# Tying a depthwise convolution's taps to fixed places in VectorE's queue

## The chip, the cores and the metric

The kernel runs on one core of one Trainium2 chip. A core has five engines that work side by side, each with its own queue that it works off in order: TensorE (matrix products; PE in the profile, PEld for its weight loads), VectorE (DVE), ScalarE (ACT), GpSimd (POOL) and SyncE (SP, which issues the DMAs here). The metric is the device time of one execution in microseconds.

## What is computed

Two layers of a block with three branches that share one input projection: sparse attention with 8 heads in 2 groups, retention with 4 heads, and a convolution. A gated sum of the three, an output projection and a feed-forward part follow. The sequence has 512 positions, the width is 1024, everything is float32. The part that the change touches is the convolution branch: 512 channels, 31 taps, causal, one weight per channel and tap.

```python
def _conv_module(a, b, dw_w, dw_b, ln_g, ln_b):
    u = a * jax.nn.sigmoid(b)
    kern = dw_w[:, None, :].astype(u.dtype)
    y = lax.conv_general_dilated(u, kern, window_strides=(1,), padding=[(CONV_WIDTH - 1, 0)],
                                 dimension_numbers=('NWC', 'WIO', 'NWC'), feature_group_count=CONV_CH)
    y = y + dw_b
    y = _layernorm(y, ln_g, ln_b)
    return jax.nn.silu(y).astype(a.dtype)
```

Between the branches stand

```python
    o_nsa = _nsa(q_n, kc, vc, ks, vs, kw, vw, g_n, ...)
    o_ret = _retention(q_r, k_r, v_r, g_r, ret_gn[l])
    o_conv = _conv_module(c_a, c_b, conv_w[l], conv_b[l], conv_ln_g[l], conv_ln_b[l])
    proj = jnp.einsum('bsnc,ncd->bsnd', br, w_branch[l])
    merged = jnp.sum(gate * proj, axis=2).astype(x.dtype)
```

## The kernel before, in words

Activations are held with features on the 128 partitions and the 512 positions along the free axis. Every product is done in a split form: a float32 operand is cut into a high part (rounded by ScalarE) and a low part (the rest, by VectorE or GpSimd), and three products replace one. `wblock` (L152) loads a weight block by DMA, ScalarE makes the high part `wh` (L144), and GpSimd the low part `wl` (L147), or VectorE in the feed-forward part (L149). All matrix products have line L108.

A layer goes through these stages:

- **Retention** (L336 to L435, "ret" pool). Queries and keys are projected (tiles `mm` and `sc`), rotated block by block on VectorE (L356 to L360, tile `rr`), transposed on TensorE and split (tile `qk`). For each of 4 heads follow: values centred on VectorE (L393 to L395, for the heads 0 and 2), scores on TensorE (tile `sc`), decay (L416, tile `rt`), the split (L111 and L112, tile `pr`), the product with the values (tile `av`), a normalisation (L428, L429) and a split (tile `bo`). After each of the first three heads `conv_input` (L303) projects the input `u` of the next of 4 convolution channel blocks; the first block is projected ahead of retention.
- **Keys** (L474 to L572). Compressed keys and values (`compress`, L482; L496 writes `XP`), the two sets of keys (L551 to L558, tile `kv`) and values (L567) of the attention.
- **Attention** (L644 to L747): 4 head pairs j, each with 2 groups g and 2 branches br, thus 16 units of 4 blocks i, 64 blocks in all. In a unit TensorE makes the scores, VectorE adds the bias and takes the minimum (L705), ScalarE the exponential (L707), VectorE scales the block by the gate over the denominator (L712, tile `s`), TensorE transposes it (L715, tile `tp`), ScalarE and VectorE split the transposed block (L720, L721, tile `pt`), and TensorE multiplies with the values (tile `av`). `more` (L736) adds independent projections between the units (`fill`: gates L444, mixes L460), queued on TensorE behind the first score product of the unit.
- **Post and feed-forward**: mixes of the three branches, output projection, then two large products.

The convolution's output is `yc`, 4 tiles of 128 channels by 512 positions. A **tap** is one VectorE instruction over 128x512 values, `yc = u shifted * weight + yc` (L333; the first tap of a channel block adds the bias, L331). There are 4 x 31 = 124 taps a layer, in a chain for each block. `conv_taps(n)` (L324) issues the next n taps whose input exists: 2 behind each of the 8 rotated blocks, 1 behind each of the 16 score splits, and 2 behind each attention block until none is left. `conv_norm` (L578) normalises the result in four pieces; `more` issues a piece a unit once no tap is left. `mix(2, OC, m)` (L767) uses it after the attention.

What sets the order: the program is built by a list scheduler that keeps, for each engine, a heap of ready instructions with the program's order as priority, and simulates a timeline. An instruction that is ready while nothing of higher priority is goes out early. So the place of `conv_taps(n)` in the program is a priority, and no place in VectorE's queue. `tc.issue_after(ins)` puts the instructions inside it behind `ins` on the queue of the engine that both use, with no wait.

Of the kernel before, what the change touches and what calls it, by code (L numbers as in the profile page):

```python
# [17 lines left out]
P = 128  # L18
# [48 lines left out]
def block_kernel(ctx: ExitStack, tc: tile.TileContext, a, out):  # L67
# [8 lines left out]

    T_ROT, T_SCORE, T_QUERY = 2, 1, 2

# [31 lines left out]
    def split(hi, lo, src, eng=None):  # L110
        nc.scalar.activation(hi, src, AF.Copy)  # L111
        (eng or nc.vector).tensor_sub(lo, src, f(hi))  # L112

# [155 lines left out]
    for l in range(DEPTH):  # L269
# [33 lines left out]
        def conv_input(c):  # L303
# [13 lines left out]
            us.append(u)  # L317

        conv_input(0)
        yc = [tl(cp, "yc", 4) for _ in range(4)]  # L320
# [25 lines left out]
        for which, c0 in (("q", 0), ("k", 2)):  # L346
# [3 lines left out]
            for i in range(NB):  # L350
                z = pz[i].rearrange("p (h s d) -> p h s d", s=2, d=32)
                cosb = cs[:, i, None, None, 0:32].to_broadcast([P, 4, 2, 32])
                sinb = cs[:, i, None, 32:64].to_broadcast([P, 4, 32])
                A = tl(rp, "rr", 8, (P, 4, 2, 32))
                B = tmp((P, 4, 2, 32))
                nc.vector.tensor_mul(A, z, cosb)  # L356
                nc.vector.tensor_mul(B[:, :, 0, :], z[:, :, 1, :], sinb)
                nc.vector.tensor_mul(B[:, :, 1, :], z[:, :, 0, :], sinb)
                nc.vector.tensor_sub(A[:, :, 0, :], A[:, :, 0, :], B[:, :, 0, :])  # L359
                nc.vector.tensor_add(A[:, :, 1, :], A[:, :, 1, :], B[:, :, 1, :])  # L360
                rr.append(A)
                conv_taps(T_ROT)
            for c in range(2):
# [19 lines left out]
        for h in range(4):  # L383
# [26 lines left out]
            for j in range(NB):  # L410
# [5 lines left out]
                nc.vector.tensor_mul(t[:, :n], s[:, :n], dec[:, :n])  # L416
                split(ph[:, at[j]], pl[:, at[j]], t[:, :n])
                conv_taps(T_SCORE)
            o = ps("av")
# [61 lines left out]
        def compress(fb, w1, w2, pe_at, is_k):  # L481
# [12 lines left out]
            for g in range(2):  # L494
                blocks = bass.AP(tensor=E.tensor, offset=E.offset + g * T, ap=[list(E.ap[0]), [2, 16], [16, NCMP]])
                nc.vector.tensor_add(XP[:, :, g, :], blocks, pe[:, :, None].to_broadcast([P, 16, NCMP]))  # L496
            w1t = []
# [49 lines left out]
        for br, fb in ((0, FB_KS), (1, FB_KW)):  # L547
# [4 lines left out]
            for g in range(2):  # L552
                nat, oth = halves(g)
                KHH[br, g], KLL[br, g] = kv(), kv()
                nc.scalar.activation(KHH[br, g][nat], t[nat], AF.Copy)
                nc.scalar.activation(KHH[br, g][oth], t[nat], AF.Copy)
                for half in (nat, oth):
                    nc.vector.tensor_sub(KLL[br, g][half], t[nat], f(KHH[br, g][nat]))  # L558
        G = tl(mix_pool, "G", 1, (P, NB, 24))
# [3 lines left out]
        for i in range(NB):  # L563
            v = kv((P, 4, P))
            zv = pz[i][:, :256].rearrange("p (c d) -> p c d", d=DH)
            nc.scalar.activation(v[:, :, 0:64], zv, AF.Copy, scale=rs4[:, i:i + 1])
            nc.vector.scalar_tensor_tensor(v[:, :, 64:128], zv, rs4[:, i:i + 1], f(v[:, :, 0:64]), op0=OP.mult,  # L567
                                           op1=OP.subtract)
            nc.scalar.activation(G[:, i, :], pz[i][:, 256:280], AF.Tanh, scale=rs4h[:, i:i + 1])
            V.append(v)  # L570
        phase.close()

# [71 lines left out]
        def attention_pair(j, tq, more):  # L644
# [43 lines left out]
            for g in range(2):  # L688
# [4 lines left out]
                for br in range(2):  # L693
# [17 lines left out]
                    for i in range(NB):  # L711
                        nc.vector.tensor_scalar(cols[i], cols[i], c[:, i:i + 1], None, op0=OP.mult)  # L712
                        pt = ps("tp")
                        for k in range(i + 1):
                            nc.tensor.transpose(pt[:, k * P:(k + 1) * P], cols[i][:, k * P:(k + 1) * P], ident)  # L715
                        for (vh, ks), (vl, _) in zip(pt_views(ph, i), pt_views(pl, i)):
# [4 lines left out]
                            nc.vector.tensor_sub(vl, src, f(vh))  # L721
                        conv_taps(T_QUERY)
                    for k, c0 in enumerate((0, 512, 896, 1152)):
# [9 lines left out]

        ON, marks, tqs = [], [], [query(0)]

        def more(j, k):  # L736
# [142 lines left out]
```

## Time and profile before

| | us |
|---|---|
| time, median of 3 runs | 1838.71 (1836.65 to 1839.05) |
| profiled execution | 1835.35 |
| its span, first to last instruction | 1833.6 |
| PE busy in the span | 1759.7 |
| DVE busy | 1162.1 |
| ACT busy | 721.4 |
| POOL busy | 512.0 |

The profiled execution lies 3.4 us below the median, and its span 1.75 us below its own time. The page lists for each engine the time in which it ran anything; a slice table cuts the span in 40 stretches of 45.8 us. A layer takes about 905 us, and its retention, keys and attention lie from 30 to 460 us in the first layer and from 930 to 1365 us in the second. "PEclk" is the share of TensorE's full clock (2.4 GHz) that was granted; 0.5 is the lower level (1.2 GHz).

### The profile page before, as it was taken

The page shows a single profiled execution, that of the slowest core. Times are in us where ns is not written, and L with a number is a line of the kernel's source. Part 1 is how long each engine was busy: PE and PEld are TensorE (multiplying, and loading weights), DVE is VectorE, ACT ScalarE, POOL GpSimd, SP SyncE. Part 2 cuts the span into 40 slices and gives each one's busy share as a digit, 9 for nine tenths or more (in the row PEclk, how much of TensorE's full clock was granted, in tenths as well). Part 3 has the DMA queues.
Part 4 walks back from the last instruction along what each step waited for, and adds up shares of the span by engine and source line. Part 5 has one row for each costly group of instructions (what it writes and reads, how often), then busy time and mean ns, then how long its engine had stood idle before and what let it go on. Part 6 is the DMA issues. An engine that isn't in the chain of part 4 may idle for free.

```text
span 1833.6 us, 23278 instructions
## 1 busy us (share of the span) xinstructions
PE 1759.7 (96%) x8592; PEld 1474.4 (80%) x8592; DVE 1162.1 (63%) x2107; ACT 721.4 (39%) x1293; POOL 512.0 (28%) x420
## 2 busy tenths in 40 slices
PE   8899899999999999999999878999999999999997
PEld 7777788888888888888897767888888888888886
DVE  7999977777554343434479998767766443434344
ACT  4423445566343232323433324555653432313231
POOL 4444433423471000000344544343235700000000
PEclk9999999999999999999999989999999999999998
DMA  4221442322653223233422113233128432232221
GB/s 165 83 74 59 130 150 94 113 87 81 229 167 104 92 92 103 92 94 102 144 81 75 65 58 129 98 110 109 69 81 268 141 97 92 93 103 92 94 91 69
DMA packets 70801, 195.82 MB, mean 107 GB/s; under 512 B 8944, under 2 KB 9328, under 8 KB 70688
## 3 DMA queue, kind: packets, MB, share of 16 engines
q1 hardware_dynamic: 70688, 194.34, 32.2%
q8 instruction: 68, 1.11, 0.2%
q14 instruction: 45, 0.37, 0.1%
HBM read 177.51 MB, written 19.42 MB: 107 GB/s over the span
## 4 chain that ended last, share of the span: by engine, by line
PE 58%; issue 21%; DVE 20%; DMA 1%; ACT 0%; SPq 0%; POOLq 0%; POOL 0%; DVEq 0%; ACTq 0%
PE mm L108 50%; DVE yc L333 9%; PE sc L108 3%; PE av L108 2%; PE tp L715 2%; DVE pr L112 1%; PE tp L108 1%; DVE rt L416 1%; DVE kv L558 1%; DVE qk L381 1%; DVE rr L359 0%; DVE t L395 0%; DVE XP L496 0%; DMA m<-in_cmp_w_k_dram 0%; DVE rr L360 0%
## 5 line engine op out<-in xcount | busy, mean ns | idle before, releaser
L108 PE MATMUL mm<-X,wh 128*128 128x512 f32 x2432 | 772.8, 396 | 17.4 <-ACT X L213 6.2
L147 POOL TENSOR_TENSOR wl<-wr,wh 128x512 fp32r<-128x512 f32 (+2 forms) x344 | 442.2, 1308 | 530.4 <-ACT wh L144 478.9
L144 ACT ACTIVATE wh<-wr 128x1024 fp32r<-128x1024 f32 (+2 forms) x301 | 296.4, 986 | 658.7 <-PE mm L108 554.1
L108 PEld LDWEIGHTS mm<-X,wh 128*128 128x128 f32 x2432 | 455.1, 190 | 108.3 <-ACT X L213 6.2
L108 PE MATMUL mm<-X,wl 128*128 128x512 f32 x1216 | 480.7, 395 | 0.2 <-DVE wl L149 0.2
L108 PEld LDWEIGHTS mm<-X,wl 128*128 128x128 f32 x1216 | 230.6, 190 | 46.8 <-DVE wl L149 0.6
L333 DVE SCALAR_TENSOR_TENSOR yc<-u,ccol,yc 128x512 f32<-128x512 f32 x240 | 227.5, 960 | 1.9
L149 DVE TENSOR_TENSOR wl<-wr,wh 128x1024 fp32r<-128x1024 f32 x129 | 158.1, 1225 | 38.6 <-ACT wh L144 38.6
L108 PE MATMUL mm<-bo,wh 128*128 128x512 f32 x512 | 163.5, 397 | 6.3 <-DVE g L444 5.8
L108 PE MATMUL mm<-fa,wh 128*128 128x512 f32 x512 | 160.2, 395 | 0.0
L796 DVE SCALAR_TENSOR_TENSOR t<-mm,rs 128x512 f32<-128x512 f32 x64 | 43.9, 691 | 161.3 <-PE mm L108 156.0
L205 POOL TENSOR_TENSOR n<-n,mhalf 128x4 f32<-128x4 f32 x15 | 18.1, 1208 | 403.8 <-DVE n L203 403.8
L226 POOL TENSOR_TENSOR t<-t,t 128x512 f32<-128x512 f32 x18 | 27.4, 1524 | 333.6 <-DVE wl L149 314.4
L108 PE MATMUL mm<-kv,wh 128*128 128x512 f32 x384 | 119.5, 389 | 0.0
L108 PEld LDWEIGHTS mm<-bo,wh 128*128 128x128 f32 x512 | 97.5, 191 | 26.8 <-DVE g L444 6.2
L108 PEld LDWEIGHTS mm<-fa,wh 128*128 128x128 f32 x512 | 96.1, 188 | 23.2
L721 DVE TENSOR_TENSOR pt<-tp,pt 128x256 fp32r<-128x256 f32 (+1 forms) x192 | 70.3, 373 | 55.2 <-ACT pt L720 54.7
L108 PE MATMUL mm<-bo,wl 128*128 128x512 f32 x256 | 101.2, 395 | 0.0
L108 PE MATMUL mm<-fa,wl 128*128 128x512 f32 x256 | 100.6, 395 | 0.0
L108 PE MATMUL mm<-wh,X 128*128 128x256 f32 (+1 forms) x480 | 94.5, 295 | 4.2 <-DVE t L307 4.2
L720 ACT ACTIVATE pt<-tp 128x256 fp32r<-128x256 f32 (+1 forms) x192 | 63.9, 343 | 86.0 <-PE tp L715 53.3
L807 DVE TENSOR_TENSOR yc<-yc,mm 128x512 f32<-128x512 f32 x32 | 22.0, 688 | 105.6 <-PE mm L108 105.6
(219 smaller groups left out, 2449.2 us busy)
## 6 DMA issues: line engine op xcount, KB each, us to landing
wr<-in_w_dram SPq DMA_DIRECT2D x128, 512.0 KB, 3.5
wr<-in_w_f_dram SPq DMA_DIRECT2D x87, 512.0 KB, 3.2
wr<-in_w_b_dram SPq DMA_DIRECT2D x48, 256.0 KB, 2.7
wr<-in_w_t_dram SPq DMA_DIRECT2D x16, 512.0 KB, 3.2
gd<-g SPq DMA_DIRECT2D x32, 256.0 KB, 2.0
g<-gd SPq DMA_DIRECT2D x32, 256.0 KB, 3.3
wr<-in_w_o_dram SPq DMA_DIRECT2D x16, 512.0 KB, 3.6
md<-g SPq DMA_DIRECT2D x16, 256.0 KB, 2.6
```

What stands on the lines that cost most here:

```text
L108: return nc.tensor.matmul(o, l, r, start=start, stop=stop)
L112: (eng or nc.vector).tensor_sub(lo, src, f(hi))
L144: nc.scalar.activation(h, t, AF.Copy)
L147: nc.gpsimd.tensor_sub(l[:, k], t[:, k], f(h[:, k]))
L149: nc.vector.tensor_sub(l, t, f(h))
L226: (nc.vector if c == KC - 1 or first_time else nc.gpsimd).tensor_add(s, s, acc)
L333: nc.vector.scalar_tensor_tensor(yc[c], x, w, yc[c], op0=OP.mult, op1=OP.add)
L715: nc.tensor.transpose(pt[:, k * P:(k + 1) * P], cols[i][:, k * P:(k + 1) * P], ident)
L720: nc.scalar.activation(vh, src, AF.Copy)
L721: nc.vector.tensor_sub(vl, src, f(vh))
L796: nc.vector.scalar_tensor_tensor(t, pf, 0.0, rs, op0=OP.max, op1=OP.mult)
L807: nc.vector.tensor_add(xT[m], xT[m], pf)
```

## The change

Every tap is now issued inside `tc.issue_after`, tied behind a VectorE instruction of its place; and the numbers differ: 1 tap behind each rotated block, 2 behind each score split, 3 behind each of 4 `XP` halves and each of the two key sets and 6 behind the last values, and the rest (`late_taps`) over the first 52 attention blocks, behind the scaled block.

```diff
-    T_ROT, T_SCORE, T_QUERY = 2, 1, 2
+    T_ROT, T_SCORE, T_KEYS, T_SLOTS = 1, 2, 3, 52
     def split(hi, lo, src, eng=None):
         nc.scalar.activation(hi, src, AF.Copy)
-        (eng or nc.vector).tensor_sub(lo, src, f(hi))
+        return (eng or nc.vector).tensor_sub(lo, src, f(hi))
+        def conv_taps_behind(ins, n):
+            with tc.issue_after(ins.ins):
+                conv_taps(n)
-                nc.vector.tensor_add(A[:, :, 1, :], A[:, :, 1, :], B[:, :, 1, :])
+                rotated = nc.vector.tensor_add(A[:, :, 1, :], A[:, :, 1, :], B[:, :, 1, :])
-                conv_taps(T_ROT)
+                conv_taps_behind(rotated, T_ROT)
-                split(ph[:, at[j]], pl[:, at[j]], t[:, :n])
-                conv_taps(T_SCORE)
+                conv_taps_behind(split(ph[:, at[j]], pl[:, at[j]], t[:, :n]), T_SCORE)
-                nc.vector.tensor_add(XP[:, :, g, :], blocks, pe[:, :, None].to_broadcast([P, 16, NCMP]))
+                laid = nc.vector.tensor_add(XP[:, :, g, :], blocks, pe[:, :, None].to_broadcast([P, 16, NCMP]))
+                conv_taps_behind(laid, T_KEYS)
-                    nc.vector.tensor_sub(KLL[br, g][half], t[nat], f(KHH[br, g][nat]))
+                    low = nc.vector.tensor_sub(KLL[br, g][half], t[nat], f(KHH[br, g][nat]))
+            conv_taps_behind(low, T_KEYS)
+        conv_taps_behind(low, 2 * T_KEYS)
-                        nc.vector.tensor_scalar(cols[i], cols[i], c[:, i:i + 1], None, op0=OP.mult)
+                        scaled = nc.vector.tensor_scalar(cols[i], cols[i], c[:, i:i + 1], None, op0=OP.mult)
-                        conv_taps(T_QUERY)
+                        slot = 4 * (4 * j + 2 * g + br) + i
+                        conv_taps_behind(scaled, late_taps * (slot + 1) // T_SLOTS - late_taps * slot // T_SLOTS)
+        late_taps = len(todo)
```

By the program's text that is 8 + 32 = 40 taps of a layer in retention, 12 + 6 + 6 = 24 in the keys, and 60 in the attention. The lines of the changed kernel stand 1 to 9 below those of before (L333 becomes L338, L712 becomes L719, L393 to L395 become L398 to L400).

VectorE's queue in the first layer, retention, where the values for head 2 are centred (`t_209` to `t_221`) while head 1 is normalised (`rt_182`). Before:

```order
L393 TENSOR_REDUCE n_210_1255<-t_209_1253 128x2
L333 SCALAR_TENSOR_TENSOR yc_50_261<-u_163_956,ccol_78,yc_50_261 128x512
L393 TENSOR_REDUCE n_214_1265<-t_213_1263 128x2
L428 TENSOR_TENSOR rt_182_1045<-rt_182_1045,tp_187_1058 128x512
L333 SCALAR_TENSOR_TENSOR yc_51_262<-u_200_1138,ccol_78,yc_51_262 128x512
L394 TENSOR_SCALAR n_210_1255<-n_210_1255 128x2
L333 SCALAR_TENSOR_TENSOR yc_50_261<-u_163_956,ccol_78,yc_50_261 128x512
L394 TENSOR_SCALAR n_214_1265<-n_214_1265 128x2
L429 SCALAR_TENSOR_TENSOR rt_182_1045<-rt_182_1045,pcol_77,gs_169_993 128x512
L333 SCALAR_TENSOR_TENSOR yc_51_262<-u_200_1138,ccol_78,yc_51_262 128x512
L395 TENSOR_TENSOR t_209_1253<-t_209_1253,n_210_1255 128x256
```

The same place now:

```order
L433 SCALAR_TENSOR_TENSOR rt_182_1045<-rt_182_1045,pcol_77,gs_169_989 128x512
L398 TENSOR_REDUCE n_210_1255<-t_209_1253 128x2
L398 TENSOR_REDUCE n_214_1265<-t_213_1263 128x2
L399 TENSOR_SCALAR n_210_1255<-n_210_1255 128x2
L399 TENSOR_SCALAR n_214_1265<-n_214_1265 128x2
L113 TENSOR_TENSOR bo_189_1066<-rt_182_1045,bo_188_1065 128x512
L400 TENSOR_TENSOR t_209_1253<-t_209_1253,n_210_1255 128x256
L400 TENSOR_TENSOR t_213_1263<-t_213_1263,n_214_1265 128x256
```

A tap stood between almost every two instructions; now none does, and the same work of head 1 and head 2 follows directly.

VectorE's queue at the first attention unit of the first layer (`s_390` is the unit's tile, `s_418` the next unit's). Before:

```order
L622 SCALAR_TENSOR_TENSOR n_395_2178<-G_350_1920,n_395_2178 128x4
L712 TENSOR_SCALAR s_390_2157<-s_390_2157,n_395_2178 128x128
L712 TENSOR_SCALAR s_390_2157<-s_390_2157,n_395_2178 128x256
L712 TENSOR_SCALAR s_390_2157<-s_390_2157,n_395_2178 128x384
L712 TENSOR_SCALAR s_390_2157<-s_390_2157,n_395_2178 128x512
L705 ISA s_418_2323,n_417_2322<-sc_420_2329,bias_374_2102 128x256
```

Now:

```order
L629 SCALAR_TENSOR_TENSOR n_395_2210<-G_350_1946,n_395_2210 128x4
L719 TENSOR_SCALAR s_390_2189<-s_390_2189,n_395_2210 128x128
L338 SCALAR_TENSOR_TENSOR yc_51_262<-u_200_1138,ccol_78,yc_51_262 128x512
L719 TENSOR_SCALAR s_390_2189<-s_390_2189,n_395_2210 128x256
L719 TENSOR_SCALAR s_390_2189<-s_390_2189,n_395_2210 128x384
L719 TENSOR_SCALAR s_390_2189<-s_390_2189,n_395_2210 128x512
L338 SCALAR_TENSOR_TENSOR yc_51_262<-u_200_1138,ccol_78,yc_51_262 128x512
L712 ISA s_418_2351,n_417_2350<-sc_420_2357,bias_374_2134 128x256
```

The attention had no tap in its queue; now a tap stands behind the first scaled block, ahead of the other three, and one ahead of the next unit's bias step, and so on through 13 of the 16 units.

VectorE's queue at the end of the keys of the first layer, where `kc` and `tq` are what the attention's first products read. Now:

```order
L573 SCALAR_TENSOR_TENSOR kv_367_2080<-av_354_1950,n_38_177,kv_367_2080 128x4x64
L336 TENSOR_SCALAR yc_51_262<-u_200_1138,ccol_78,pcol_77 128x512
L338 SCALAR_TENSOR_TENSOR yc_50_261<-u_163_952,ccol_78,yc_50_261 128x512
L338 SCALAR_TENSOR_TENSOR yc_51_262<-u_200_1138,ccol_78,yc_51_262 128x512
L338 SCALAR_TENSOR_TENSOR yc_50_261<-u_163_952,ccol_78,yc_50_261 128x512 x7
L525 TENSOR_SCALAR kc_307_1699<-tp_306_1697 64x31
L526 TENSOR_SCALAR kc_307_1699<-tp_306_1697 64x31
L338 SCALAR_TENSOR_TENSOR yc_50_261<-u_163_952,ccol_78,yc_50_261 128x512 x4
L648 SCALAR_TENSOR_TENSOR tq_372_2129<-mm_371_2104,rs_39_179 128x512
```

Fourteen taps stand between the last values and `tq`; before, all taps of the layer were done ahead of the last values, and `kc` and `tq` followed each other.

On TensorE, ScalarE, GpSimd and SyncE the same instructions are issued. TensorE's attention units start within some 30 products of where they did; in the retention the order changes by a few products at a time.

## Rows read from the trace of the kernel before

**Rows 1.** The page: busy time by engine, DVE by slice, the chain's lines.

```profile
PE 1759.7 (96%) x8592; PEld 1474.4 (80%) x8592; DVE 1162.1 (63%) x2107; ACT 721.4 (39%) x1293; POOL 512.0 (28%) x420
...
DVE  7999977777554343434479998767766443434344
...
PE mm L108 50%; DVE yc L333 9%; PE sc L108 3%; PE av L108 2%; PE tp L715 2%; DVE pr L112 1%; PE tp L108 1%; DVE rt L416 1%; DVE kv L558 1%; DVE qk L381 1%; DVE rr L359 0%; DVE t L395 0%; DVE XP L496 0%; DMA m<-in_cmp_w_k_dram 0%; DVE rr L360 0%
```

**Rows 2.** By stretch: length; PE, PEld, DVE, ACT, POOL busy us; PE clock; DMA.

```profile
30.00:210.00 180.00, 159.27 (x868) 137.14 (x867) 175.03 (x264) 58.67 (x95) 80.02 (x57) 0.94 0.20 69
210.00:240.00 30.00, 28.39 (x177) 24.54 (x175) 26.88 (x37) 15.16 (x27) 17.58 (x13) 1.00 0.73 230
240.00:420.00 180.00, 177.35 (x939) 150.61 (x938) 132.91 (x428) 103.27 (x261) 61.27 (x55) 0.99 0.30 101
420.00:460.00 40.00, 40.00 (x204) 33.61 (x204) 28.54 (x71) 22.86 (x51) 13.22 (x11) 1.00 0.24 84
390.00:420.00 30.00, 28.25 (x157) 24.00 (x156) 25.88 (x94) 19.58 (x52) 6.55 (x5) 0.94 0.19 65
930.00:1110.00 180.00, 158.44 (x887) 137.15 (x886) 175.52 (x265) 58.19 (x94) 82.66 (x57) 0.95 0.20 70
1110.00:1140.00 30.00, 23.57 (x147) 21.23 (x145) 27.07 (x35) 13.47 (x25) 15.01 (x11) 0.89 0.40 143
1140.00:1320.00 180.00, 177.85 (x930) 150.70 (x930) 129.08 (x410) 100.60 (x252) 58.94 (x53) 0.99 0.30 99
```

**Rows 3.** The taps of L333 by stretch: DVE busy us (taps).

```profile
30.00:210.00 180.00, 98.78 (x109) 0.94 0.20 69
210.00:240.00 30.00, 13.05 (x12) 1.00 0.73 230
930.00:1110.00 180.00, 105.22 (x109) 0.95 0.20 70
```

**Rows 4.** What TensorE waited for, 30 to 210 us: total, times, longest.

```profile
PE av L108 <- DVE pr L112: 8.7, 6, 3.4
PE mm L108 <- DVE t L307: 4.1, 2, 2.6
PE mm L108 <- DVE g L444: 2.9, 1, 2.9
```

**Rows 5.** VectorE around one such wait: start, length, idle before.

```profile
183.36 3.45 DVE L333 SCALAR_TENSOR_TENSOR yc<-u,ccol,yc 128x512 f32<-128x512 f32 x2
186.73 1.34 DVE L112 TENSOR_TENSOR pr<-rt,pr 128x128 fp32r<-128x128 f32 x1
```

**Rows 6.** TensorE at that place.

```profile
188.13 0.69 PE L108 MATMUL av<-pr,v 128*128 128x128 f32 x2 [3.43 <-DVE pr L112]
```

**Rows 7.** All taps of L333: shortest, median, longest ns.

```profile
L333 DVE SCALAR_TENSOR_TENSOR yc<-u,ccol,yc x240: 730/744/1815, 34.8 to 1132.6; 128x512 f32<-128x512 f32 x120
```

**Rows 8.** What VectorE waited for, 240 to 420 us: total, times, longest.

```profile
DVE pt L721 <- ACT pt L720: 15.4, 16, 4.5
```

**Rows 9.** VectorE in the attention, two places.

```profile
271.62 0.42 DVE L721 TENSOR_TENSOR pt<-tp,pt 128x256 fp32r<-128x256 f32 x1
...
394.88 3.32 DVE L712 TENSOR_SCALAR s<-s,n 128x128 f32<-128x128 f32 x4
398.12 0.41 DVE L721 TENSOR_TENSOR pt<-tp,pt 128x256 fp32r<-128x256 f32 x1
```

**Rows 10.** TensorE at the same two places.

```profile
273.81 0.86 PE L108 MATMUL av<-pt,kv 128*128 128x512 f32 x4
...
398.59 0.98 PE L108 MATMUL av<-pt,kv 128*128 128x512 f32 x4 [1.62 <-DVE pt L721]
```

**Rows 11.** GpSimd's low parts of the weights, 240 to 420 us: busy, mean ns.

```profile
L147 POOL TENSOR_TENSOR wl<-wr,wh 128x512 fp32r<-128x512 f32 (+1 forms) x50 | 59.6, 1214 | 106.7 <-ACT wh L144 99.5 <-PE tp L715 3.6 <-PE sc L108 1.9
```

**Rows 12.** The convolution's normalised output, 400 to 520 us: first and last start.

```profile
L108 PE MATMUL mm<-yc,wh x32: 392/393/399, 496.2 to 517.6; 128*128 128x512 f32 x32
...
L111 ACT ACTIVATE yc<-u x4: 614/632/634, 433.6 to 445.3; 128x512 fp32r<-128x512 f32 x4
```

More of the change, by code (lines that the diff above doesn't have):

```diff
@@ L566, in block_kernel @@
             nc.scalar.activation(v[:, :, 0:64], zv, AF.Copy, scale=rs4[:, i:i + 1])
-            nc.vector.scalar_tensor_tensor(v[:, :, 64:128], zv, rs4[:, i:i + 1], f(v[:, :, 0:64]), op0=OP.mult,
-                                           op1=OP.subtract)
+            low = nc.vector.scalar_tensor_tensor(v[:, :, 64:128], zv, rs4[:, i:i + 1], f(v[:, :, 0:64]), op0=OP.mult,
+                                                 op1=OP.subtract)
             nc.scalar.activation(G[:, i, :], pz[i][:, 256:280], AF.Tanh, scale=rs4h[:, i:i + 1])
             V.append(v)
+        conv_taps_behind(low, 2 * T_KEYS)
         phase.close()
```

## The prediction

> **What bounds the kernel now.** I read the busy time by engine first, then the busy time by stretch, then the taps and TensorE's waits in those stretches, then single places. TensorE is busy 96% of the span and VectorE 63% [rows 1], so over the whole kernel TensorE is the bound. The slices say that this mean hides two different halves: VectorE stands at 9 tenths in the slices of each layer's retention, and lower afterwards. The chain of waits names one VectorE line above all others, the taps, with 9% [rows 1], which is far more than a chain through TensorE alone would give to a line that fills gaps.
>
> By stretch [rows 2] the picture is this. In the first layer's retention (30 to 210 us) VectorE is busy 175.0 of 180 us, 97%, and TensorE only 159.3. In the attention (240 to 420 us) VectorE is busy 132.9, 74%, and TensorE 177.4. The second layer repeats it: 175.5 and 158.4, then 129.1 and 177.9. So VectorE is the bound in retention, TensorE in attention. All taps lie on the wrong side of that line: 109 of a layer's 120 plain taps run in the 180 us of retention and take 98.8 and 105.2 us there, 12 in the next 30 us, in the keys (one lies across the border), and that is all of them, so none in the attention [rows 3].
>
> What TensorE loses in retention has two parts. Idle: 180 - 159.3 = 20.7 us and 180 - 158.4 = 21.6 us. Clock: a mean granted clock of 0.94 and 0.95 with two levels of 1 and 0.5 is 10.8 and 9.0 us of work not done, and the dips come beside the waits (attention, with few waits, has 0.99). Together 31.5 and 30.6 us. The waits are for VectorE [rows 4]: for the low parts of the scores 8.7 us, for the projected convolution input 4.1, for a gate 2.9. One place shows how: two taps run from 183.36 for 3.45 us, the low part of a score is queued behind them at 186.73 [rows 5], and TensorE's product stands idle for 3.43 us until 188.13 [rows 6].
>
> **The change part by part.** No instruction is added or removed on any engine: 124 taps a layer stay. They move. By the text, retention holds 40 afterwards, the keys 24, the attention 60.
>
> *Retention.* A plain tap in the first layer's retention costs 98.78 / 109 = 0.906 us [rows 3]. VectorE's load there falls from 175.0 to 175.0 - 98.8 + 40 x 0.906 = 112 us (the four first taps of the blocks are left out), against TensorE work of 180 - 31.5 = 148 us: 76%, about the attention's 74% now. At 74% TensorE loses 2.7 us idle and 1.8 us clock of 180 [rows 2], 4.5 in all. Retention has shorter chains between the engines than the attention (a rotated block, its transpose and its split follow each other with little beside them), and 2 taps now follow each score split, ahead of the next one. So I leave it 10 us of its loss a layer, and gain 31.5 - 10 + 30.6 - 10 = 42 us. Bounds: all but 4.5 a layer, 53 us; or two thirds of the loss staying, 20 a layer, 22 us.
>
> *Keys.* 24 taps instead of 12 in a stretch where VectorE is at 27 of 30 us [rows 2]; but the 12 there now are a queue carried over from retention, which would be gone. Fourteen taps stand ahead of `tq`, which the attention's first product reads. At 0.9 us that is 12.6 us, beside a compression chain that waits for its own DMA and TensorE in the first layer; in the second, TensorE already loses 6.4 us idle and 3.3 of clock there. I take a loss of 4 us for both layers, with bounds of a 6 us gain (the second layer's idle goes) and a 12 us loss.
>
> *Attention.* This is what speaks against the change. The queue is in order: a tap behind the first scaled block holds up the other three, their transposes on TensorE, the split of the next block, and the next unit's bias step, whose product buffers (two `sc`) TensorE waits to reuse. VectorE's idle there is 180 - 132.9 = 47.1 us and 50.9 us [rows 2], its largest part waits for ScalarE's half of a block's split, 15.4 us in the first layer [rows 8]. Sixty taps must fit. Their price: the median tap takes 0.744 us, the longest 1.815 [rows 7]; the mean 0.906 belongs to a stretch where GpSimd is busy 80.0 of 180 us, and in the attention it is busy 61.3. Scaling the excess of 0.162 us by 61.3/80.0 gives 0.87 us a tap, 52.2 us. VectorE then needs 185.1 and 181.3 us for what fitted into 180. Where it is the bound it reached 97.2% (175.03 of 180), so the stretches would take 190.4 and 186.5 us: 10.4 + 6.5 = 17 us lost. Bounds: every tap at 0.744 us makes 177.5 and 173.7, thus 182.6 and 178.7, a loss of 2.6 us; every tap at the 1.09 us of the first layer's keys (13.05 / 12) [rows 3] makes 198.3 and 194.5, thus 204.0 and 200.1, a loss of 44 us.
>
> That there is little room is seen in single places. At 271.62 a low part is done 1.8 us before TensorE's product at 273.81 uses it; at 398.12, behind four scaled blocks that took 3.32 us, there is no room at all, and TensorE waits 1.62 us [rows 9, 10]. In that 30 us stretch VectorE is at 25.9, 86%, and TensorE has 1.75 us idle and a clock of 0.94 [rows 2], so the loss sets in well short of 97%.
>
> In this trace a tap that is slowed takes at most 1.815 - 0.744 = 1.07 us longer [rows 7], less than one of GpSimd's low-part instructions (1.21 us mean) [rows 11]. The Trainium skill, "SBUF — State Buffer", section "SBUF: two separate sides", says that VectorE instructions with two SBUF inputs and GpSimd instructions that read SBUF share a port pair under an exclusive lock, which the one that starts first keeps for its whole length. The trace agrees in size. By that rule a tap in the attention would find the port taken 34% of the time (61.3 of 180) and wait half an instruction, 0.744 + 0.34 x 0.61 = 0.95 us, a loss of 27 instead of 17 us; the sum would be 1826, inside this case's range.
>
> *Normalisation.* The last tap falls in unit 12, so the four pieces of the normalisation come one unit later, in units 12 to 15. Its output is written from 433.6 to 445.3 and first read at 496.2 [rows 12]: 50 us of cover, a unit lasts about 13. I cost it at nothing; VectorE has 11 us spare between 420 and 460 for it.
>
> **Sum.** 1835.35 (the profiled execution) - 42 + 4 + 17 = 1814. The profiled execution stands 3.4 us below the median of the runs, 1838.71, to which the same change would give 1818. I take 1816, from a base of 1837 between the two, a gain of 1.1%.
>
> **The rivals.**
>
> *The attention takes the taps free* (chance 0.20). Its 47 us of idle absorb the 45 us that 60 undisturbed taps take, and the scheduler places TensorE's products later to suit. For it: the scheduler knew of the taps when it laid the attention. Against it: the place at 398 us. Time: 1837 - 42 + 4 + 3 = 1802, and 1791 if retention loses only 4.5 us a layer, 1781 if the keys win 6 besides.
>
> *The attention becomes bound by VectorE* (0.20), the other side: in-order taps between the scaled blocks, each meeting GpSimd's work, cost TensorE more than retention gives back. Its place is the 13 units with taps, its price 1.04 us a tap or more: there the two stretches need 132.9 + 129.1 + 120 x 1.04 = 386.8 us of VectorE, at 97.2% 398 us for 360, a loss of 38, which is all that is won (42 - 4). At 1.09 us and with a retention gain of only 30 the time is 1837 - 30 + 4 + 44 = 1855. For it: taps in the keys cost that now. Against it: GpSimd is less busy in the attention than in retention and keys.
>
> *The taps were not what held TensorE* (0.12). If two thirds of retention's loss come from chains that stay (a gain of 22 us), then with 4 and 17 lost nothing is left: 1837 - 22 + 21 = 1836. For it: two taps after each split still stand ahead of the next split. Against it: nearly every wait is for VectorE, at 97% busy.
>
> The forecast has 0.48, with its own range of 1804 to 1829.
>
> **How the numbers follow.** Without either of the outer tails, 8 in 10 lie between 1787 and 1848. A measurement of this kernel tells 0.2%, 3.7 us, from no change. Faster holds the forecast, the free attention and a little of the third rival: 0.48 + 0.20 + 0.03 = 0.71. The same: 0.08, from the third and the edge of the second. Slower: 0.21.
>
> **What would show it.** In the profile after, by stretch: VectorE in retention at about 75% with TensorE's idle and clock loss near 10 us instead of 31; the waits for `pr`, `t` of L307 and `g` gone or short; retention some 20 us shorter in each layer. In the attention VectorE at 95% or more, new TensorE waits for `pt` and `s`, and each attention 5 to 12 us longer. I am wrong if TensorE's retention loss stays over 20 us a layer, or if the attention's length does not change (the first rival) or grows by more than 19 us a layer (the second).

## The result and the profile after

The changed kernel takes 1807.3 us (median, 1804.6 to 1807.3) against 1838.5 us before in the same comparison: ratio 0.983, 95% interval 0.981 to 0.985, a gain of 1.7%. The forecast was 1816.

The page of the changed kernel, busy time by engine, DVE by slice and the lines of the chain, answers to [rows 1]:

```profile
PE 1756.8 (97%) x8592; PEld 1473.4 (82%) x8592; DVE 1137.4 (63%) x2107; ACT 720.4 (40%) x1293; POOL 501.2 (28%) x420
...
DVE  6976989997454344434459778899866443434344
...
PE mm L109 55%; DVE yc L338 4%; PE av L109 2%; PE sc L109 2%; PE tp L109 1%; DVE s L719 1%; PE tp L722 1%; DVE pt L728 1%; DVE s L712 1%; DVE g L448 1%; DVE qk L386 1%; DMA wr<-in_w_f_dram 0%; ACT s L714 0%; DVE kv L563 0%; DVE rr L364 0%
```

PE's busy time has hardly changed (1759.7 before); it is the span around it that shrank. The taps (now L338) fall from 9% to 4% of the chain, and the row of 9s in VectorE's slices moves from retention into the keys and the attention.

By stretch, first retention, keys and attention of layer 1, then of layer 2 (columns as in [rows 2]; the stretches are cut where the stages now lie):

```profile
30.00:187.00 157.00, 152.09 (x877) 133.67 (x876) 118.30 (x194) 60.60 (x97) 72.46 (x58) 0.98 0.25 80
187.00:224.00 37.00, 32.29 (x203) 28.37 (x202) 36.33 (x50) 13.93 (x27) 15.51 (x12) 0.95 0.64 200
224.00:415.00 191.00, 183.70 (x935) 153.52 (x935) 175.98 (x495) 106.01 (x267) 65.62 (x55) 0.97 0.28 93
917.00:1073.00 156.00, 155.23 (x931) 138.30 (x930) 117.07 (x198) 62.91 (x101) 74.39 (x59) 1.00 0.30 96
1073.00:1109.00 36.00, 33.95 (x199) 31.72 (x199) 34.41 (x52) 12.84 (x27) 16.36 (x13) 0.86 0.33 105
1109.00:1300.00 191.00, 182.95 (x926) 152.54 (x925) 173.42 (x488) 104.75 (x261) 65.03 (x54) 0.97 0.28 90
```

I read TensorE's loss from such a row as in the prediction: idle time plus length times (1 - clock). The clock has two digits, so the second part is good to about 1 us. First retention: 157 - 152.09 = 4.9 and 0.02 x 157 = 3.1, 8.0 us instead of 31.5 in the 180 us before. Second retention: 0.8 instead of 30.6. Keys: 4.7 + 1.9 = 6.6 (1.6 before), and 2.1 + 5.0 = 7.1 (9.7 before). Attention: 7.3 + 5.7 = 13.0 and 8.1 + 5.7 = 13.8; before 4.5 and 4.0 in 180 us.

The taps alone, same stretches of the first layer and the second attention, as in [rows 3], and all of them, as in [rows 7]:

```profile
30.00:187.00 157.00, 33.48 (x38) 0.98 0.25 80
187.00:224.00 37.00, 21.14 (x23) 0.95 0.64 200
224.00:415.00 191.00, 51.26 (x59) 0.97 0.28 93
1109.00:1300.00 191.00, 51.33 (x59) 0.97 0.28 90
```

```profile
L338 DVE SCALAR_TENSOR_TENSOR yc<-u,ccol,yc x240: 730/747/1830, 35.7 to 1284.2; 128x512 f32<-128x512 f32 x120
```

A tap costs 51.26 / 59 = 0.87 us in the attention.

What TensorE waited for in the changed kernel, in 30 to 187 us (two rows), 184 to 225, 224 to 415 and 430 to 490 us (total, times, longest), as in [rows 4]:

```profile
PE av L109 <- DVE pr L113: 2.8, 2, 1.8
PE tp L371 <- DVE rr L365: 2.1, 2, 1.5
...
PE mm L109 <- ACT G L575: 4.7, 1, 4.7
...
PE sc L109 <- DVE n L712: 5.3, 5, 2.7
...
PE mm L109 <- ACT os L112: 1.1, 1, 1.1
```

The waits for `t` and `g` are gone from retention and those for `pr` fall from 8.7 to 2.8 us. What has grown is the attention's wait of score products for the bias instruction (L712), which has to empty one of two `sc` buffers. Before, in 240 to 420 us, it was

```profile
PE sc L108 <- DVE n L705: 0.2, 1, 0.2
```

Where stages begin and end is read from two tiles: score products of the attention and the products that read the convolution's output (the last numbers of a row's head are first and last start). Before:

```profile
L108 PE MATMUL sc<-kv,QS x128: 222/337/551, 244.4 to 439.2; 128*128 128x128 f32 x32, 128*128 128x256 f32 x32, 128*128 128x384 f32 x32, 128*128 128x512 f32 x32
...
L108 PE MATMUL sc<-kv,QS x128: 222/337/562, 1149.7 to 1344.9; 128*128 128x128 f32 x32, 128*128 128x256 f32 x32, 128*128 128x384 f32 x32, 128*128 128x512 f32 x32
...
L108 PE MATMUL mm<-yc,wh x32: 392/393/398, 1401.9 to 1423.3; 128*128 128x512 f32 x32
```

After:

```profile
L109 PE MATMUL sc<-kv,QS x128: 221/338/690, 224.3 to 428.1; 128*128 128x128 f32 x32, 128*128 128x256 f32 x32, 128*128 128x384 f32 x32, 128*128 128x512 f32 x32
...
L109 PE MATMUL mm<-yc,wh x32: 392/393/398, 487.2 to 509.5; 128*128 128x512 f32 x32
...
L109 PE MATMUL sc<-kv,QS x128: 221/337/686, 1109.2 to 1313.0; 128*128 128x128 f32 x32, 128*128 128x256 f32 x32, 128*128 128x384 f32 x32, 128*128 128x512 f32 x32
...
L109 PE MATMUL mm<-yc,wh x32: 387/393/398, 1373.9 to 1395.3; 128*128 128x512 f32 x32
```

With the first layer's 496.2 before [rows 12] this gives a balance of the two profiled executions:

| us | first layer | second layer |
|---|---|---|
| up to the first score product (in layer 2 from layer 1's first `yc` product: 653.5 before, 622.0 after) | -20.1 | -31.5 |
| first to last score product (before 194.8, 195.2; after 203.8, 203.8) | +9.0 | +8.6 |
| last score product to first `yc` product (before 57.0, 57.0; after 59.1, 60.9) | +2.1 | +3.9 |

Together -51.6 + 17.6 + 6.0 = -28.0 us, and 1835.35 - 28.0 is the 1807.3 of the profiled execution after.

### The profile page after: what moved, and what is told of

It reads as the page before. It is cut to its first block, busy times and chain, and to the rows that moved or that the text cites. A ratio compares the mean times of both kernels' runs of the same rounds, so it can differ in the third digit from the quotient of the medians.

```text
span 1805.5 us, 23271 instructions
## 1 busy us (share of the span) xinstructions
PE 1756.8 (97%) x8592; PEld 1473.4 (82%) x8592; DVE 1137.4 (63%) x2107; ACT 720.4 (40%) x1293; POOL 501.2 (28%) x420
## 4 chain that ended last, share of the span: by engine, by line
PE 63%; issue 20%; DVE 14%; ACT 1%; DMA 1%; POOL 0%; SPq 0%; POOLq 0%; DVEq 0%; ACTq 0%
PE mm L109 55%; DVE yc L338 4%; PE av L109 2%; PE sc L109 2%; PE tp L109 1%; DVE s L719 1%; PE tp L722 1%; DVE pt L728 1%; DVE s L712 1%; DVE g L448 1%; DVE qk L386 1%; DMA wr<-in_w_f_dram 0%; ACT s L714 0%; DVE kv L563 0%; DVE rr L364 0%
## 5 line engine op out<-in xcount | busy, mean ns | idle before, releaser
L148 POOL TENSOR_TENSOR wl<-wr,wh 128x512 fp32r<-128x512 f32 (+2 forms) x344 | 436.6, 1292 | 565.8 <-ACT wh L145 532.1
L338 DVE SCALAR_TENSOR_TENSOR yc<-u,ccol,yc 128x512 f32<-128x512 f32 x240 | 213.9, 893 | 1.7
L727 ACT ACTIVATE pt<-tp 128x128 fp32r<-128x128 f32 (+1 forms) x192 | 63.9, 342 | 87.8 <-PE tp L722 55.6
L714 ACT ACTIVATE s<-s,n 128x128 f32<-128x128 f32 (+3 forms) x128 | 71.6, 560 | 62.2 <-DVE n L712 61.5
L109 PE MATMUL mm<-wh,X 128*128 128x256 f32 (+1 forms) x480 | 90.2, 286 | 0.0
```

What stands on the lines that cost most here:

```text
L109: return nc.tensor.matmul(o, l, r, start=start, stop=stop)
L148: nc.gpsimd.tensor_sub(l[:, k], t[:, k], f(h[:, k]))
L338: nc.vector.scalar_tensor_tensor(yc[c], x, w, yc[c], op0=OP.mult, op1=OP.add)
L714: nc.scalar.activation(s, s, AF.Exp, scale=-1.0, bias=mx[:, i:i + 1], accum_out=den[:, i:i + 1])
L727: nc.scalar.activation(vh, src, AF.Copy)
```

## The experiments

My theory: in retention the taps stood between VectorE's short instructions that TensorE waits for, and an in-order queue made TensorE wait; moving them into the attention costs less there. Rivals: the number of taps in a stage (VectorE's load) decides, wherever they stand in the queue; or retention's loss had other causes. Runs with numbers as edits change the tuple `T_ROT, T_SCORE, T_KEYS, T_SLOTS = 1, 2, 3, 52`. "Taps" are given as retention / keys / attention in the first layer; the changed kernel has 40 / 24 / 60.

**The new counts without the tie.**

```diff
-            with tc.issue_after(ins.ins):
-                conv_taps(n)
+            conv_taps(n)
```

> The changed kernel's counts of taps (1, 2, 3 and the rest over 52 blocks), without the tie. Its queue holds 114 taps of a layer in retention, 10 in the keys, none in the attention, as before. If the load of VectorE in each stage decides: 1838 us, within 4 of the kernel before. If the counts work as priorities by themselves: between 1810 and 1830.

Measured: 1840.4 us, ratio 1.001 (0.9996 to 1.003): no change from before. The queue holds 114 / 10 / 0 taps, as before. The numbers alone do nothing: untied, the taps are ready early and go out early. In 30 to 210 us VectorE is at 174.0 us and TensorE at 156.6, near the 175.0 and 159.3 of [rows 2]. Since the queue stayed as it was, this run does not tell the load of VectorE from the place of the taps.

**The tie with the old counts.** Taps 32 / 0 / 92, 2 behind each of 46 attention blocks.

```diff
+    T_ROT, T_SCORE, T_KEYS, T_SLOTS = 2, 1, 0, 46
-  conv_taps_behind(scaled, late_taps * (slot + 1) // T_SLOTS - late_taps * slot // T_SLOTS)
+  conv_taps_behind(scaled, 2)
```

> The tie kept, with the counts of before (2 behind a rotated block, 1 behind a split, 2 behind each attention block until none is left): 32 taps of a layer in retention, none in the keys, 92 over 46 attention blocks. If load decides: 11.5 units are 135 us, VectorE's own work there 100, and 92 taps at 0.87 are 80, together 180 us, at 97.2% 185, so each attention is 50 us longer than before instead of 9, less 4 us a layer won in retention and keys: about 1880. If it is the place in the queue that decides (no tap ahead of a chain's instructions) and not the number: 1807 to 1817.

Measured: 1832.2 us, 0.997 (0.9955 to 0.998). Both expectations missed. The first score product comes at 215.1, 29 us earlier than before, but the attention lasts 229.5 us, 34.7 more. The same 191 us as above, which in that run begin 9 us into the attention:

```profile
224.00:415.00 191.00, 172.01 (x820) 142.39 (x819) 181.88 (x469) 92.42 (x235) 60.69 (x47) 0.90 0.26 85
```

and its longest waits of TensorE:

```profile
PE tp L722 <- DVE pt L728: 9.3, 2, 6.4
PE sc L109 <- DVE n L712: 4.2, 2, 3.9
```

Here VectorE is the bound: 95% busy, TensorE 19.0 us idle and 19.1 us of clock lost. So the rival that I gave 0.20 exists, at 92 taps. By the prediction's own formula these would have cost more: 132.9 + 92 x 0.87 = 212.9 us of VectorE, at 97.2% 219 us for 180, 39 us, and 35 us in the second layer, where 32.0 were measured.

**Late taps cut to 8 columns.** Same instructions and places, nearly no time in them; the rest of each late tap's sum is left out. In the edit, cut short here, `late` is the first 8 columns for the taps issued in the attention and all 512 for the others.

```diff
-  nc.vector.scalar_tensor_tensor(yc[c], x, w, yc[c], op0=OP.mult, op1=OP.add)
+  nc.vector.scalar_tensor_tensor(yc[c][:, late], x[:, late], w, yc[c][:, late], op0=OP.mult, op1=OP.add)
```

> The changed kernel, with the 60 taps of a layer in the attention cut from 512 to 8 columns (the rest of their sums is left out), so each still stands in its place and costs next to nothing. If the attention's loss is these taps' time on VectorE: the attention falls back to 188 us, 9 less a layer, and what comes late behind it (2 us a layer) goes too: 1785, between 1783 and 1790. If the loss comes from something else that the new order brought (the clock, the fillers' places): 1800 or more.

Measured: 1785.9 us, 0.971 (0.969 to 0.973), as expected. The attention's row:

```profile
224.00:415.00 191.00, 186.88 (x974) 157.59 (x972) 144.61 (x511) 108.02 (x278) 63.53 (x56) 0.99 0.29 95
```

The loss falls from 13.0 to 4.1 + 1.9 = 6.0 us, and first to last score product takes 196.7 and 196.2 us, 1 to 2 more than before. So it is the time that the taps take on VectorE that costs in the attention; as many instructions tied at the same places cost next to nothing when they are short. Whether full taps would cost less at other places this run does not tell. The cost is 21 us for 120 taps, 0.18 us each of the 0.87 that they take. The rest is hidden.

**More taps in retention.** Tied, 91 / 23 / 10.

```diff
+    T_ROT, T_SCORE, T_KEYS, T_SLOTS = 3, 5, 3, 52
```

> The tie kept, but 3 taps behind a rotated block and 5 behind a split: 91 taps of a layer in retention, about 21 in the keys, about 12 in the attention. If load decides: retention's VectorE work rises from 112 by 51 x 0.9 to 158 us, at 97.2% 163 us, with the chains 168 against 157 now and 180 before, so 10 to 12 us a layer are lost again and 8 to 10 are won in the attention: 1805 to 1818. If place decides: retention as now, attention as before: 1786 to 1790. If a dense tie is as bad as none: 1835.

Measured: 1824.5 us, 0.992 (0.990 to 0.994), slower than the expectation by load (1805 to 1818) and faster than a dense tie as bad as none (1835). Retention's row:

```profile
30.00:210.00 180.00, 166.40 (x951) 144.68 (x949) 169.99 (x257) 68.67 (x108) 86.48 (x63) 0.96 0.26 85
```

VectorE is at 170.0 of 180 us, 94%, and TensorE loses 13.6 + 7.2 = 20.8 us, two thirds of the 31.5 of before. That speaks for the load as the larger part; how much of the other third is the tie, and how much the 18 plain taps fewer in these 180 us (91 against 109), this run does not tell, and no run ties as many taps in retention as there were before.

**One tap more behind each score split.** Taps 56 / 23 / 45.

```diff
+    T_ROT, T_SCORE, T_KEYS, T_SLOTS = 1, 3, 3, 52
```

> The changed kernel with 3 taps behind each score split instead of 2: 56 taps of a layer in retention, 20 to 23 in the keys, 45 to 48 in the attention. If each stage loses in proportion to its taps (retention and keys 0.29 us a tap between 64 and about 112 taps, attention 0.16 us a tap between none and 60): 1807 + 2 x (4 - 2) = 1811. If the attention's loss is steep at its end, as between 60 and 92 taps (0.69 us a tap), and so falls by 9 us a layer: 1797.

Measured: 1800.9 us, 0.9798 (0.978 to 0.9815). The interval touches that of the change, so the gain of some 6 us is not settled; it lies nearer to the second figure, by the steep end. In the profiled execution the second attention is 4.4 us shorter than in the changed kernel and the stretch ahead of it 6.1 longer.

**Late taps over all 64 blocks.**

```diff
+    T_ROT, T_SCORE, T_KEYS, T_SLOTS = 1, 2, 3, 64
```

> The changed kernel with the 60 late taps spread over all 64 attention blocks instead of 52: 3.75 a unit instead of 4.6, and the convolution's normalisation wholly behind the attention. If VectorE's load in the units decides: attention 2 to 4 us shorter a layer, the normalisation hidden by the 50 us before its output is read: 1800 to 1804. If that cover is gone once it starts behind the attention: TensorE waits for the normalisation's four steps in the mixes, 5 to 15 us a layer: 1815 to 1835.

Measured: 1813.7 us, 0.987 (0.985 to 0.988): slower than the change by about 7 us, and just under the range for a cover that is gone. The rows of the attention and of what follows:

```profile
224.00:408.00 184.00, 180.72 (x921) 151.13 (x921) 161.01 (x471) 101.41 (x258) 65.34 (x57) 0.99 0.30 99
408.00:455.00 47.00, 40.07 (x184) 31.90 (x183) 35.15 (x87) 21.50 (x54) 7.20 (x6) 0.85 0.32 106
```

The attention gets better (5.1 us lost in 184) and the end pays: 6.9 us idle and 7.1 us of clock in the 47 us behind it. By the program's text the last taps now stand in the last unit, so the normalisation starts behind it, with no unit left beside which it could run. TensorE's longest waits in 408 to 500 us are for the last unit's own transposed blocks, which now share VectorE with the last taps and the normalisation:

```profile
PE tp L722 <- DVE pt L728: 3.7, 4, 1.4
PE av L109 <- ACT pt L727: 1.8, 3, 0.7
```

**Late taps behind the low part of the transposed block** instead of behind the scaled block.

```diff
-    scaled = nc.vector.tensor_scalar(cols[i], cols[i], c[:, i:i + 1], None, op0=OP.mult)
+    nc.vector.tensor_scalar(cols[i], cols[i], c[:, i:i + 1], None, op0=OP.mult)
-    nc.vector.tensor_sub(vl, src, f(vh))
+    cut = nc.vector.tensor_sub(vl, src, f(vh))
-  conv_taps_behind(scaled, late_taps * (slot + 1) // T_SLOTS - late_taps * slot // T_SLOTS)
+  conv_taps_behind(cut, late_taps * (slot + 1) // T_SLOTS - late_taps * slot // T_SLOTS)
```

> The changed kernel, the same 60 late taps over the same 52 blocks, but each tied behind the low part of its block's transposed values instead of behind its scaled block, so that no tap stands between the four scaled blocks. If the load decides and not the place: 1807, within 3. If the loss in the attention comes from taps ahead of the scaled blocks and the next bias step (TensorE waits 5.3 and 4.6 us there): 1797 to 1800.

Measured: 1801.8 us, 0.980 (0.9785 to 0.982), between the two; the interval touches that of the change. The wait of the score products falls from 5.3 to 2.1 us, but the granted clock of the attention is 0.96 instead of 0.97, which takes 1.9 us of it back; first to last score product takes 207.4 us, 3.6 more, and the stretch behind it 55.5, 3.6 less.

**Three edits together** (3 behind each split, 64 blocks, behind the low part).

```diff
+    T_ROT, T_SCORE, T_KEYS, T_SLOTS = 1, 3, 3, 64
+  conv_taps_behind(cut, late_taps * (slot + 1) // T_SLOTS - late_taps * slot // T_SLOTS)
```

> Three taps behind a split, the late taps over 64 blocks, and each behind the low part: the three edits of this set together. If load alone decides: the sum of what the first two show, 1804 to 1808. If the place and the steep end of the attention both count: 1785 to 1795.

Measured: 1836.9 us, 0.9994 (0.998 to 1.0005): all of the gain is gone, against both figures. The attentions are 5 us shorter than in the change (198.8 and 198.4 us), yet from the last score product to the first `yc` product it takes 77.1 and 78.9 us instead of 59.1 and 60.9: 18 us more in each layer. The 40 us behind the first attention, and the wait that was not there before, for a step of the normalisation (L601):

```profile
415.00:455.00 40.00, 26.57 (x126) 20.69 (x125) 29.89 (x70) 18.60 (x44) 6.52 (x5) 0.81 0.32 106
```

```profile
PE mm L109 <- DVE u L601: 4.8, 1, 4.8
```

**The first and the last edit without the second** (3 behind each split, behind the low part, 52 blocks).

```diff
+    T_ROT, T_SCORE, T_KEYS, T_SLOTS = 1, 3, 3, 52
+  conv_taps_behind(cut, late_taps * (slot + 1) // T_SLOTS - late_taps * slot // T_SLOTS)
```

> Base: the changed kernel, 1807.3 us. Two edits together: 3 taps behind each score split instead of 2, and the late taps tied behind the low part of the transposed block instead of the scaled block; the normalisation of the convolution stays inside the attention, over 52 blocks. The two edits alone gave 1800.9 and 1801.8. If they act on different waits (the first by fewer taps in the attention, the second by where a tap stands behind the scaled blocks) the gains of 6.4 and 5.5 us add: 1795, between 1792 and 1798. Rival: both relieve the same wait, of the score products for the bias and minimum instructions: 1800 to 1803. Second rival: what cost 35 us with all three edits together came from these two and not from starting the normalisation behind the attention: 1815 to 1840.

Measured: 1806.5 us, 0.982 (0.980 to 0.9835): no better than the change. So it was the 64 blocks that cost 30 us in the run before, beside the other two edits; alone they cost about 7. The two small gains do not add, and not even one of them is left, against all three of my figures; after this I take no difference below 0.4% between these kernels for shown.

**The same without taps in the keys.** Taps 56 / 0 / 68.

```diff
+    T_ROT, T_SCORE, T_KEYS, T_SLOTS = 1, 3, 0, 52
```

> Base: the kernel with the two edits above; here no tap is tied in the keys, so that 23 and 20 taps of the two layers move from the keys into the attention (68 there in both layers). Theory by exposed cost: a late tap costs 21.5 us over 120 taps (the run with narrow late taps), 0.18 us each, so the 43 taps add 8 us to the attentions, and the keys give back at most the 4.9 us for the gate, some 2 us of other waits and the lowered clock (0.95 and 0.86 in the two stretches of some 37 us), 5 to 10 us in all: within 4 us of the kernel beside it. Rival by density: 46 blocks with 2 taps each (92 taps) lengthened an attention by 31 us against 9.4 us with 60 taps, 0.68 us for each tap more, which makes 43 taps 29 us, less the 5 to 10 of the keys: 19 to 24 us slower than the kernel beside it.

Measured: 1802.3 us, 0.9795 (0.977 to 0.982), 4 us under the kernel beside it with intervals that overlap, about what the theory by exposed cost allows; the one by density fails at 68 taps.

**The taps of the keys to retention.** 64 / 0 / 60, otherwise as the change.

```diff
+    T_ROT, T_SCORE, T_KEYS, T_SLOTS = 2, 3, 0, 52
```

> Base: the changed kernel, 1807.3 us. The 24 taps of the keys go to retention (2 behind each rotated block, 3 behind each score split: 64 of a layer), none is tied in the keys; the attention keeps its 60 at the same places. Theory of the keys: taps there cost TensorE 4.7 us idle and 1.6 of clock in 185 to 224 us, 2.1 and 5.2 in 1070 to 1110 us, 13.5 in all, which go, while retention (VectorE 118 of 157 us, 75%, then 118 + 24 x 0.88 = 139, 89%) gives up 1 to 3 us a layer: 1796 to 1800. Rival by retention's load: at 94% (91 taps) TensorE lost 20.8 us of the first layer's retention instead of 8; at 89% some 6 us more a layer: 1804 to 1808, no gain.

Measured: 1803.4 us, 0.981 (0.980 to 0.982), nearer to the rival. Its rows for the keys of the first layer (the same 37 us as above) and for retention of the second:

```profile
187.00:224.00 37.00, 36.72 (x234) 32.44 (x233) 19.79 (x46) 16.57 (x32) 14.58 (x14) 1.00 0.69 220
...
917.00:1070.00 153.00, 148.28 (x854) 129.81 (x853) 134.44 (x213) 56.79 (x91) 73.12 (x56) 0.99 0.24 78
```

The keys lose 0.3 us instead of 6.6, so the taps were what cost there. But the second retention, with VectorE at 134.4 of 153 us, 88%, now loses 4.7 + 1.5 = 6.2 instead of 0.8. The first retention, at 87%, loses 8.1 as with the change, so the rival's 6 us came in one layer only.

**The taps of the keys to the attention.** 40 / 0 / 84.

```diff
+    T_ROT, T_SCORE, T_KEYS, T_SLOTS = 1, 2, 0, 52
```

> Base: the changed kernel, 1807.3 us. The 24 taps of the keys go to the attention (84 of a layer over 52 blocks), retention keeps its 40. The keys give back 13.5 us at most. Theory that a late tap's price is steady, 0.18 us each as with the narrow late taps: 47 taps add 8.5 us: 1802. Rival that the attention has a knee: TensorE lost (idle and clock) 31 us in both attentions with 68 taps a layer and 72 us with 92, which between them makes 58 us with 84, against 27 now: 31 more, less 13.5: 1825.

Measured: 1819.1 us, 0.989 (0.988 to 0.991), nearer to the knee. The attention (212 to 415 us):

```profile
212.00:415.00 203.00, 188.81 (x936) 155.20 (x935) 187.19 (x515) 103.58 (x266) 66.41 (x53) 0.95 0.27 89
```

Loss 14.2 + 10.2 = 24.4 us. In the first attention, then, some 190 to 200 us of it, it is 6.0 us with narrow taps, 13.0 with 60, 24.4 with 84 and 38.1 with 92: the first 60 cost 7 us, the next 32 cost 25. The second attention goes the same way: 5.3, 13.8, 27.6 and 33.0 us in stretches of 191 to 218 us.

## Why the prediction came out

*Retention* was right in mechanism and too small in size. VectorE's load was forecast at 112 us beside 148 us of TensorE's work, 76%; it is 118.30 us beside 157 - 8.0 = 149, 79% (75% of the stretch, the measure by which the attention had 74%). I left TensorE 10 us of loss a layer. It keeps 8.0 in the first, most of that in one stretch, 60 to 90 us, where its loss hardly changed (6.6 before, 6.2 after). The row of before, then of after:

```profile
60.00:90.00 30.00, 26.73 (x119) 22.13 (x120) 29.53 (x46) 11.75 (x22) 14.23 (x12) 0.89 0.18 57
```

```profile
60.00:90.00 30.00, 27.07 (x121) 22.09 (x122) 27.08 (x43) 12.90 (x24) 11.77 (x11) 0.89 0.23 80
```

In the second layer it keeps 0.8. So the gain by loss is 23.5 + 29.8 = 53 us, not 42: at my upper bound, which came from the attention's own loss at that load. That the sum meets this bound is luck, since the layers lie on both sides of its 4.5. My reason for leaving more, shorter chains between the engines, weighed nothing in the second layer. The rival that the taps were not what held TensorE has fallen: with 40 taps instead of 114 the loss went from 31.5 to 8.0 and from 30.6 to 0.8, and with 91 it was back at 20.8. What sets the loss at 60 to 90 us in the first layer alone is open. It is not the number of taps there: with 13 before it was 6.6 us, with 10 now 6.2, and with 14 in the run with the keys' taps in retention 3.2.

*Keys*: forecast a loss of 4, measured by loss 6.6 + 7.1 - 1.6 - 9.7 = 2.4 us. The two layers do what I wrote with the signs apart: the first loses 5, the second wins 2.6. What I missed is the room: without taps there the keys lose nearly nothing, as the run with the keys' taps in retention shows. VectorE, at 36.33 of 37 us, has no room left there.

*Attention*: forecast 17, measured 17.6 us between the first and the last score product, at the forecast price, 0.87 us a tap. The estimate of 0.95 us by the lock rule of the Trainium skill, "SBUF — State Buffer", section "SBUF: two separate sides", was too high. The size is right and the reasoning only half, so that the agreement is in part luck: VectorE is at 92% and not at the 95% or more that I named as the sign, so it was not the bound that my formula took it for. The waits for `pt` that I named stay short (0.9, 0.3 and 0.2 us in 224 to 415 us); the score products' 5.3 us are the largest. Nearly half of the loss is clock, 5.7 of 13.0 us; the idle part comes in single places (the 5.3 us are five waits), and where I looked a tap is in the way. The longest of the five in the changed kernel (start, length, engine, instruction, idle before):

```profile
386.34 2.95 POOL L148 TENSOR_TENSOR wl<-wr,wh 128x512 fp32r<-128x512 f32 x2 [7.74 <-PE sc L109]
386.47 1.70 DVE L338 SCALAR_TENSOR_TENSOR yc<-u,ccol,yc 128x512 f32<-128x512 f32 x1
...
388.09 1.22 DVE L629 SCALAR_TENSOR_TENSOR n<-G,n 128x4 f32<-128x4 f32 x1
389.23 0.55 DVE L712 CUSTOM_DVE_ANT_0 s<-sc,bias 128x384 f32<-128x384 f32 x1
...
389.84 0.44 PE L109 MATMUL sc<-kv,QS 128*128 128x128 f32 x2 [2.72 <-DVE n L712]
```

A tap starts just behind GpSimd and takes 1.70 us, then an instruction over 4 columns takes 1.22, the bias step comes at 389.23 only, and TensorE waits 2.72 us for its buffer. The formula that fitted at 60 taps overstates the loss at 92 (39 and 35 us against 34.7 and 32.0), and it had no part for the gradual loss below the bound.

*The attention taken for free* (1802) and *the attention bound by VectorE* (1855) are the two ends of what the runs with 60, 84 and 92 late taps show. At 60 taps the cost is hidden to four fifths (0.18 of 0.87 us a tap). With 84 that has turned: first to last score product takes 220.7 us in the first layer, 16.9 more for 24 taps, 0.70 us each.

*Normalisation*: its own cover holds. Its output is written and first read like this in the changed kernel:

```profile
L109 PE MATMUL mm<-yc,wh x32: 392/393/398, 487.2 to 509.5; 128*128 128x512 f32 x32
...
L112 ACT ACTIVATE yc<-u x4: 614/632/633, 428.9 to 441.1; 128x512 fp32r<-128x512 f32 x4
```

46 us lie between the last write and the first read, 51 before. Yet the stretch behind the attention grew by 2.1 and 3.9 us, for which I had no term: my attention ended with the last score product, and the late taps' cost does not. The narrow taps bring the stretch back to 58.1 and 57.3 us, so 1.0 and 3.6 us of it are the taps'. The main wait that shows there is for `os`, the split output of the attention (1.1 us). In the run with taps behind the low part the stretch is 3.6 us shorter and the attention as much longer, so I count the two as one cost: 23.6 us where I had 17. The runs with 64 blocks show that the 50 us were no measure of the cover. There the output is still written 29 and 31 us ahead of its first read, in the first layer, and yet the stretch is 10 to 18 us a layer longer than in the change. TensorE waits earlier, for the last unit's blocks and for steps of the normalisation. That what covers the normalisation is the attention units beside which its pieces run is my reading of these rows.

*Sum*: the terms were -42 + 4 = -38 up to the attention and +17 from there, and came out as -51.6 and +23.6. Two terms were too small in size, by 14 and 7 us on opposite sides, so that the time is 7 us under the forecast's 1814 for the profiled execution. That they lie on opposite sides is luck. The step that failed most is the 10 us a layer left in retention.

No version tried is clearly better than the change: 56 / 23 / 45, 56 / 0 / 68, 64 / 0 / 60 and the late taps behind the low part lie 4 to 6 us lower, with intervals that overlap its own.

## What to carry to other kernels

In a queue worked off in order, filler work costs by what stands behind it: put it where the engine has slack in that stage, not where it first becomes ready, and tie it there, since changed counts alone left the queue as it was. Spread it so that this engine keeps room in every stage. In the first retention TensorE lost 8.0 us with VectorE at 75%, 8.1 at 87% and 20.8 at 94%. But the busy share alone does not tell the loss: in the second retention it went from 0.8 to 6.2 us between 75% and 88%, and in the first attention it was 13.0 us with 60 taps and 24.4 with 84, with VectorE at 92% in both. And look at what follows the filler: here it had to end early enough that the preparation of its result still had other work beside it.

## What was not expected of the hardware

In some stretches short waits cost about twice their length. In the attention with 92 late taps TensorE was idle 19.0 us of 191 and lost as much again to a granted clock of 0.90, a mean over the two levels, 2.4 and 1.2 GHz; with narrow taps it was idle 4.1 us at a clock of 0.99. And an instruction over 128x4 values took 1.22 us beside GpSimd's low parts, where it took 0.15 us 1.6 us later:

```profile
389.71 0.15 DVE L629 SCALAR_TENSOR_TENSOR n<-G,n 128x4 f32<-128x4 f32 x1
```

The slow one ends at 389.31, and GpSimd's pair at 389.29. The Trainium skill, "SBUF — State Buffer", section "SBUF: two separate sides", says that VectorE instructions with two SBUF inputs and GpSimd instructions that read SBUF share a port pair under an exclusive lock. This place agrees with that: the small instruction took about as long as one of GpSimd's two low parts (2.95 us for both).
